# First four k-rows of x joined with three tiles' weights, and the last product summed onto a residual held in its banks

## The chip, the core and the metric

One core of one Trainium2 chip runs the kernel. The metric is the device time of one execution in microseconds (us). The kernel before takes 1969.95 us, the median of 3 runs (1969.86 to 1970.58). The profile is of one execution of its own, which took 1970.17 us; the span that the profile shows of it is 1968.4 us. Engines are named as in the profile: PE is TensorE's matmul, PEld its weight load, DVE VectorE, ACT ScalarE, POOL GpSimd, SP SyncE, which here only issues DMAs.

## What is computed

A hybrid encoder layer on 512 positions of 2048 channels: a norm, one input projection that feeds a convolution group and a 2-D neighbourhood attention, an output projection, and a gated MLP with a width-3 convolution, each with its residual; then a final norm.

```python
xn = rms_norm(x, attn_norm_g[l])
proj = jnp.einsum("bsd,dc->bsc", xn, w_in[l])
u_val, u_gate, q, k, v = jnp.split(proj, split_pts, axis=-1)
y_conv = conformer_conv(u_val, u_gate, conv_dw_w[l], conv_dw_b[l], conv_ln_g[l], conv_ln_b[l])
y_na = neighborhood_attention(heads(q), heads(k), heads(v), rpb[l])
...
x = x + jnp.einsum("bsc,cd->bsd", mixed, w_out[l])
xn = rms_norm(x, ffn_norm_g[l])
up = depthwise_conv(jnp.einsum("bsd,df->bsf", xn, w_up[l]), ffn_dw_w[l], ffn_dw_b[l])
gate, val = jnp.split(up, 2, axis=-1)
x = x + jnp.einsum("bsf,fd->bsd", jax.nn.silu(gate) * val, w_down[l])
...
return rms_norm(x, final_norm_g)
```

## The kernel before

Everything is float32. Each product is made of float32r matmuls of 128 x 128 weights against 512 moving columns. An operand is split into a high part (a copy cast to float32r, ACT) and a low part (the difference, DVE), and three matmuls, high by high, high by low and low by high, make one block's product. Weights come as units of 128 x 1024 (8 blocks, 512 KB): `raw_unit` loads one by a DMA from SP into one of 9 `raw` buffers, and `parts` splits it into `whi` (L136, ACT) and `wlo` (L137, DVE), 4 buffers each. `weights()` hands the units out in the order of the list `plan`, and makes them 3 ahead of their use.

The stages follow one another on PE: the 16 gate and value tiles and the attention's q, k and v tiles (`project`, L153 to L156, 48 matmuls a tile), the output projection (`out_half`), the up-projection (`up`, L745) and the down-projection (`product2`, L884). The last two are 2 x 2 block products in seven multiplications each.

**The start.** The input is scaled by `attn_norm_g` alone; the norm's factor `rstd` comes later and is multiplied onto the projected tiles. `first_glu` makes the first gate tile and the first value tile at once, in two PSUM banks, while x and the weights still arrive. x comes in 16 k-rows of 128 channels, the weights of the two tiles (`w_0`) in six pieces of 1, 1, 2, 4, 4 and 4 k-rows. SP issues x; ACT's own DMA queue brings the scale `g1` and the first three weight pieces (`we`), ahead of ACT's first instruction. Per k-row, `split_x` makes `xh` (L273, ACT) and `xl` (L274, DVE), and per piece `piece` makes the weights' two parts (L284, or L136 and L137). `pin` keeps these in the order of the code, so the order of the DMAs and splits at the start is written by hand. Ahead of it 11 matmuls of ones by ones (`WARM`, L124) run on PE. Then come the next gate tile's two units (`early`), and x once more with positions on partitions (`xn`, 8 loads of 512 KB), which ACT squares (L315) for the norm; `prm`, all other parameters, is loaded last. The norm's factor is a chain on DVE and ACT (`root_steps`) with two matmuls on PE at its end (`st`, L255).

**The end.** The last product (`product2(5, ...)`) makes the first half of the positions of half the columns, in four banks, i = 0 to 3: bank i holds rows i // 2 (128 positions each) and columns i % 2 (512 each). 18 of its 22 units run bank by bank within a unit; the last 4 units (`TAIL`) run bank after bank, 12 matmuls for each. Behind each bank `ready` adds it to `e3`, which holds the residual and the other products' shares (L935, DVE), squares the sum (L937, ACT) and multiplies by the final gain (L939, DVE; for i = 1 and 3, `fused`, the gain is left to `write`). Behind banks 1 and 3 `write` makes the norm's factor of 128 positions (L953 to L957), multiplies the four tiles with it (L963 on ACT, L965 and L967 on DVE) and issues their DMAs (L969). A scheduler orders instructions by priority within what the code's dependences allow; `shifted(-100)` moves this part ahead.

## Time and profile before

| | |
|---|---|
| time, median of 3 runs | 1969.95 us (1969.86 to 1970.58) |
| the profiled execution | 1970.17 us, span 1968.4 us |
| PE busy | 1956.4 us, 99% |
| PEld, DVE, ACT, POOL busy | 1665.2, 1608.1, 1100.9, 225.3 us |
| chain that ended last | PE 98% of the span |
| HBM read, written | 427.12 MB, 111.15 MB |

A row of the timeline gives the start (us from the span's start), the time from the first instruction's start to the last one's end, the engine, the line, the operation, the tile written and the tile read, and how many instructions were merged; in brackets how long the engine had been idle, and who ended that. A matmul's shown end lies behind the point at which the next one starts, so a run of n matmuls is as long as n - 1 starts and one duration. A row of the waits gives the total, the number and the longest of the waits. A row of a table of windows gives each engine's busy time and number of instructions in the stretch, then the granted clock, the DMA engines' busy share and the rate of their transfers. In answers on one tile or line, "DMA to landing" is the time from a transfer's issue until its semaphore says that all has arrived.

### The profile page before, as it was taken

To read this page: it belongs to the slowest core of one execution; us is meant where nothing else is said; L and a number is where in the kernel's file an instruction comes from. 1 tells how busy PE (TensorE), PEld (TensorE's weight loads), DVE (VectorE), ACT (ScalarE), POOL (GpSimd) and SP (SyncE) were. 2 spreads that over 40 slices of the span, in tenths; PEclk is the share of its full clock that TensorE was granted. 3 is DMA by queue.
4 is the path that set the end of the run, shared out by engine and by line. 5 is a ranking of instruction groups with operands and counts; after the bars stand their busy time and mean duration, and the time that the engine had idled before them with its cause. 6 is when DMAs were issued, how large, how long until landed. Compare 5 with 4: busy or idle time off the path is not lost.

```text
span 1968.4 us, 27634 instructions
## 1 busy us (share of the span) xinstructions
PE 1956.4 (99%) x10125; PEld 1665.2 (85%) x10125; DVE 1608.1 (82%) x2339; ACT 1100.9 (56%) x1766; POOL 225.3 (11%) x310
## 2 busy tenths in 40 slices
PE   9999999999999999999999999999999999999998
PEld 7888888888888888888888888888888888888886
DVE  5987687798557889898989898888888898885765
ACT  6244424448526666666666666666666644554654
POOL 0111111111001111111111111111110400000000
PEclk9999999999999999999999999999999999999999
DMA  9776766676858899999999999999986977666563
GB/s 363 182 196 173 187 178 185 179 190 203 258 147 213 206 251 244 271 246 272 236 274 245 268 242 269 242 270 246 265 229 168 387 242 233 217 214 193 192 201 120
DMA packets 141817, 447.83 MB, mean 228 GB/s; under 512 B 15088, under 2 KB 27632, under 8 KB 140272
## 3 DMA queue, kind: packets, MB, share of 16 engines
q1 hardware_dynamic: 88880, 290.31, 43.4%
q0 software_dynamic: 42624, 148.92, 35.3%
q10 hardware_dynamic: 10176, 6.83, 1.1%
q8 instruction: 80, 1.31, 0.3%
q14 instruction: 57, 0.47, 0.1%
HBM read 427.12 MB, written 111.15 MB: 273 GB/s over the span
## 4 chain that ended last, share of the span: by engine, by line
PE 98%; DVE 1%; DMA 0%; issue 0%; ACT 0%; ACTq 0%; DVEq 0%
PE pu L745 44%; PE pd L884 21%; PE pj L153 7%; PE pj L154 7%; PE pj L156 7%; PE po L153 3%; PE po L154 3%; PE po L156 3%; PE po L538 1%; PE sc L495 1%; PE pj L369 1%; PE trp L521 1%; DMA we<-in_w 0%; PE trx L640 0%; PE pj L373 0%
## 5 line engine op out<-in xcount | busy, mean ns | idle before, releaser
L136 ACT ACTIVATE whi<-raw 128x1024 fp32r<-128x1024 f32 x573 | 605.0, 1057 | 543.3 <-PE pj L154 154.7
L137 DVE TENSOR_TENSOR wlo<-raw,whi 128x1024 fp32r<-128x1024 f32 x573 | 699.3, 1221 | 235.4 <-ACT whi L136 196.3
L745 PE MATMUL pu<-xc,whi 128*128 128x512 f32 x2464 | 593.6, 391 | 0.0
L745 PEld LDWEIGHTS pu<-xc,whi 128*128 128x128 f32 x2464 | 451.3, 188 | 86.7 <-DVE xc L633 0.4
L745 PEld LDWEIGHTS pu<-xc,wlo 128*128 128x128 f32 x2464 | 319.2, 191 | 13.7
L745 PE MATMUL pu<-xc,wlo 128*128 128x256 f32 x2464 | 324.2, 283 | 0.0
L884 PE MATMUL pd<-whi,ho 128*128 128x512 f32 x1232 | 305.1, 389 | 0.1
L884 PEld LDWEIGHTS pd<-whi,ho 128*128 128x128 f32 x1232 | 231.1, 188 | 48.7 <-DVE vl L758 0.5
L153 PE MATMUL pj<-xh,whi 128*128 128x512 f32 x608 | 238.9, 393 | 0.0
L154 PE MATMUL pj<-xl,whi 128*128 128x512 f32 x608 | 236.8, 389 | 0.0
L395 DVE SCALAR_TENSOR_TENSOR y<-ch,prm,y 128x500 f32<-128x500 f32 (+14 forms) x240 | 177.2, 742 | 5.3
L884 PE MATMUL pd<-wlo,ho 128*128 128x512 f32 x616 | 165.1, 389 | 0.0
L156 PE MATMUL pj<-xh,wlo 128*128 128x512 f32 x608 | 150.3, 389 | 0.0
L153 PEld LDWEIGHTS pj<-xh,whi 128*128 128x128 f32 x608 | 114.1, 188 | 26.7 <-issue 2.8
L884 PEld LDWEIGHTS pd<-wlo,ho 128*128 128x128 f32 x616 | 115.6, 188 | 24.0
L156 PEld LDWEIGHTS pj<-xh,wlo 128*128 128x128 f32 x608 | 114.1, 188 | 23.7
L154 PEld LDWEIGHTS pj<-xl,whi 128*128 128x128 f32 x608 | 114.2, 188 | 23.5 <-issue 0.2
L754 ACT ACTIVATE pu<-pu 128x512 f32<-128x512 f32 x132 | 76.5, 580 | 92.9 <-PE pu L745 92.8
L694 POOL DMA_DIRECT2D raw<-in_w_up x88 | 78.0, 887 | 366.1 <-DVE wlo L137 143.9
L208 POOL DMA_DIRECT2D ws<-in_w_down x88 | 79.5, 903 | 301.5 <-DMA ws<-in_w_down 126.6
L205 POOL DMA_DIRECT2D ws<-ws x44 | 23.0, 524 | 317.9 <-PE pj L156 105.1
L205 POOL DMA_DIRECT2D ws<-in_w_down x44 | 23.2, 528 | 306.9 <-PE pj L156 174.5
(193 smaller groups left out, 1967.8 us busy)
## 6 DMA issues: line engine op xcount, KB each, us to landing
raw<-in_w_up SPq DMA_DIRECT2D x220, 512.0 KB, 5.9
ws<-in_w_down POOLq DMA_DIRECT2D x132, 512.0 KB, 6.3
raw<-in_w_up POOLq DMA_DIRECT2D x88, 512.0 KB, 7.3
raw<-ws SPq DMA_DIRECT2D x88, 512.0 KB, 3.6
raw<-in_w_in SPq DMA_DIRECT2D x76, 512.0 KB, 5.2
raw<-in_w_down SPq DMA_DIRECT2D x66, 512.0 KB, 4.1
ws<-ws POOLq DMA_DIRECT2D x44, 512.0 KB, 5.8
raw<-in_w_out SPq DMA_DIRECT2D x32, 512.0 KB, 4.7
```

Source lines behind the costliest of these rows:

```text
L136: i = nc.scalar.activation(hi[:, :n], raw[:, :n], AF.Copy)
L137: j = nc.vector.tensor_sub(lo[:, :n], raw[:, :n], hi[:, :n].bitcast(F32))
L153: nc.tensor.matmul(ps, hi, mh, start=first and k == 0, stop=False)
L154: nc.tensor.matmul(ps, hi, ml, start=False, stop=False)
L156: i = nc.tensor.matmul(ps, lo[:, wk * P:(wk + 1) * P], mh, start=False, stop=last and k == len(ws) - 1)
L205: behind(nc.gpsimd.dma_start(wsum[c][k], a), ins)
L208: nc.gpsimd.dma_start(wsum[c][k], w_down[k, {1: A21, 2: A11, 4: A11, 6: A12}[c]], accum_op=ALU.add, max_dma_last_dim=ROW)
L395: nc.vector.scalar_tensor_tensor(y[:, a:b], h[:, a + j - PAD:b + j - PAD], prm[:, o:o + 1], y[:, a:b], op0=ALU.mult, op1=ALU.add)
L694: nc.gpsimd.dma_start(a[c], w_up[f, q2], accum_op=ALU.add)
L745: i = nc.tensor.matmul(ps[:, :n], part[:, k * P:(k + 1) * P], comb[c][k][:, :n], start=j == 0 and not more, stop=j == 2 * U - 1, skip_grou ...
L754: nc.scalar.activation(to, ps, AF.Copy)
L884: m = nc.tensor.matmul(ps[i], h[:, o + t * P:o + (t + 1) * P], w[:, d], start=start and not more and kind == 0 and j == 0, stop=stop and k ...
```

## The change

The name of the change speaks first of narrow edge blocks in the attention. They stand in both kernels (`EDGE`, `KEYS`, `ATEDGE`), and the difference between the two holds nothing of the attention. It holds two things.

**The start.** `first_glu` makes three tiles at once, gate 0, value 0 and gate 1, the third in a bank of the pool that `project` uses; `glu(1)` then only projects its value tile. For the first four k-rows (`ROWS`) one array `xw` joins x's row, the three tiles' weights of that row and, in the first, the scale: one DMA each from SP (467 KB, then 459 KB three times). ACT issues no DMA at the start. The first row's splits are shared out: ACT makes half of `xh` and two tiles of `weh`, DVE the other half and one tile, and DVE copies the scale out. The other twelve k-rows come in pieces of two. Five of the eight `xn` loads and their squares stand among these pieces instead of behind them. Only the third tile's separate units (1 MB) fall away as such; value 1's two units are the `early` ones now. `WARM` is 8 instead of 11. `gated(0, ...)` is called at the end of `first_glu`, not behind the next unit.

**The end.** `prime` copies the four tiles of `e3` into four PSUM banks (ACT) during the product before, and the last product adds to what is there (`more` is True). `ready` then squares the bank itself (ACT) and multiplies the bank by the gain (DVE); the addition (L935) is gone for these four. `write` takes the primed bank for the fused tiles, and goes through the columns upwards.

```diff
-WARM = 11
+WARM = 8
+ROWS = 4
...
-    nc.scalar.dma_start(g1, par[:, :KD])
-    cuts = (0, 1, 2, 4, 8, 12, 16)
-    first = []
-    for k0, k1 in zip(cuts[:3], cuts[1:4]):
-        first.append(t2("we")[:, :2 * (k1 - k0) * P])
-        nc.scalar.dma_start(first[-1], w_0[:, 2 * k0 * P:2 * k1 * P])
...
+    for k in range(ROWS):
+        n = 3 * P
+        both = t4([P, S + n + KD], "xw")
+        m = S + n + (0 if k else KD)
+        pin(nc.sync.dma_start(both[:, :m], xw[k][:, :m]))
+        x, raw, lo = both[:, :S], both[:, S:S + n], t2("wel", F32R)[:, :n]
+        if k:
+            split_x(k, x)
+            his = [t2("weh", F32R)[:, :n]]
+            pin(nc.scalar.activation(his[0], raw, AF.Copy))
         else:
...
+            g = both[:, S + n:S + n + 1]
+            pin(nc.scalar.activation(h[:, :H], x[:, :H], AF.Copy, scale=g))
+            pin(nc.vector.tensor_copy(his[0], raw[:, :P]))
+            pin(nc.vector.tensor_scalar(h[:, H:], x[:, H:], g, None, op0=ALU.mult))
+            pin(nc.scalar.activation(his[1], raw[:, P:], AF.Copy))
+            pin(nc.vector.tensor_copy(g1, both[:, S + n:]))
+            pin(nc.vector.scalar_tensor_tensor(l, x, g, h.bitcast(F32), op0=ALU.mult, op1=ALU.subtract))
...
+    for p in range(ROWS // 2, KD // 2):
         x = t4([P, 2 * S], "x")
         pin(nc.sync.dma_start(x, xT[p]))
         for k in range(2):
             split_x(2 * p + k, x[:, k * S:(k + 1) * S])
...
+        piece(2 * p, 2 * p + 2)
+        if p > 2:
+            square(*todo.pop(0))
...
-        two = [psa.tile([P, S], F32, tag="tr", name="pj", bufs=2) for _ in range(2)]
+        three = [psa.tile([P, S], F32, tag="tr", name="pj", bufs=2) for _ in range(2)]
+        three.append(psm.tile([P, S], F32, tag="mm", name="pj"))
...
-        late.append(lambda: gated(0, *two))
+        gate.append(three[2])
+        gated(0, *three[:2])
...
-            add(x[i], x[i], ps[i])
+            if not whole:
+                add(x[i], x[i], ps[i])
+            src = ps[i] if whole else x[i]
             q = t2("sq")
-            nc.scalar.activation(q, x[i], AF.Square, accum_out=sq[th][:, t, o:o + 1])
+            nc.scalar.activation(q, src, AF.Square, accum_out=sq[th][:, t, o:o + 1])
             if i not in fused:
-                nc.vector.tensor_mul(x[i], x[i], gs[d])
+                nc.vector.tensor_mul(x[i], src, gs[d])
...
+    def prime(x):
+        primed.extend(four(True))
+        for a, b in zip(x, primed):
+            nc.scalar.activation(b, a, AF.Copy)
             yield
...
-                    nc.vector.scalar_tensor_tensor(x, x, y, gs[d], op0=ALU.mult, op1=ALU.mult)
+                    nc.vector.scalar_tensor_tensor(x, primed[i], y, gs[d], op0=ALU.mult, op1=ALU.mult)
...
-    steps += [ready(e0, a, 0, 1), ready(e1, a, 1, 1)]
+    steps += [ready(e0, a, 0, 1), ready(e1, a, 1, 1), prime(e3)]
...
-    a = four(True)
-    for i in product2(5, a, False):
+    for i in product2(5, primed, True):
```

How the order of instructions changes is shown at two places. The first is the start. SP's DMAs of before, from the first on (`raw<-in_w` are the two tiles' weights, `xn` the input once more):

```order
L292 DMA x<-in_xT 128x512 x2
L297 DMA x<-in_xT 128x1024 x2
L130 DMA raw<-in_w 128x1024
L297 DMA x<-in_xT 128x1024 x2
L130 DMA raw<-in_w 128x1024
L297 DMA x<-in_xT 128x1024 x2
L130 DMA raw<-in_w 128x1024
L297 DMA x<-in_xT 128x1024
L130 DMA raw<-in_w_in 128x1024
L309 DMA xn<-in_xn 128x1024 x4
```

SP's DMAs of the change, from the first on:

```order
L295 DMA xw<-in_xw 128x912
L295 DMA xw<-in_xw 128x896 x3
L320 DMA x<-in_xT 128x1024
L125 DMA raw<-in_w 128x768
L320 DMA x<-in_xT 128x1024
L125 DMA raw<-in_w 128x768
L286 DMA xn<-in_xn 128x1024
L320 DMA x<-in_xT 128x1024
L125 DMA raw<-in_w 128x768
L286 DMA xn<-in_xn 128x1024
```

The weights of the first rows, which came on ACT's queue, stand in SP's now, in one transfer with x, and the first `xn` stands ninth where it stood fourteenth. On PE, before, the first rows (`pj` are the projected tiles' banks, `weh` and `wel` the first weights' parts):

```order
L124 MATMUL warm<-ones 128x128 x11
L369 MATMUL pj<-xh,weh 128x512 x2
L369 MATMUL pj<-xl,weh 128x512 x2
L373 MATMUL pj<-xh,wel 128x512 x2
L369 MATMUL pj<-xh,weh 128x512 x2
L369 MATMUL pj<-xl,weh 128x512 x2
L373 MATMUL pj<-xh,wel 128x512 x2
```

PE's first rows of the change:

```order
L119 MATMUL warm<-ones 128x128 x8
L387 MATMUL pj<-xh,weh 128x512 x3
L387 MATMUL pj<-xl,weh 128x512 x3
L391 MATMUL pj<-xh,wel 128x512 x3
L387 MATMUL pj<-xh,weh 128x512 x3
L387 MATMUL pj<-xl,weh 128x512 x3
L391 MATMUL pj<-xh,wel 128x512 x3
```

Each k-row gives PE nine matmuls where it gave six, and three matmuls of ones are gone ahead of them. The second place is the end. DVE's last rows of before, from the last unit's split on (`xr` are the output's tiles, `pd` the banks):

```order
L935 TENSOR_TENSOR xr<-xr,pd 128x512
L954 TENSOR_SCALAR rsv<-sq,rsm 128x1
L955 SCALAR_TENSOR_TENSOR rsv<-rsr,rsv 128x1
L956 RECIPROCAL rsv<-rsv 128x1
L957 TENSOR_SCALAR rsy<-rsv,rsr 128x1
L965 SCALAR_TENSOR_TENSOR xr<-xr,rsy,g_15496 128x512
L967 TENSOR_SCALAR xr<-xr,rsy 128x512
```

DVE's last rows of the change:

```order
L975 TENSOR_SCALAR rsm<-rsm 128x1
L983 TENSOR_SCALAR rsv<-sq,rsm 128x1
L984 SCALAR_TENSOR_TENSOR rsv<-rsr,rsv 128x1
L985 RECIPROCAL rsv<-rsv 128x1
L986 TENSOR_SCALAR rsy<-rsv,rsr 128x1
L996 TENSOR_SCALAR xr<-xr,rsy 128x512
L994 SCALAR_TENSOR_TENSOR xr<-pd,rsy,g_15503 128x512
```

The addition of the last bank is gone ahead of the chain, and the two multiplications behind it have changed places. PE's last rows of before (banks 0 and 1 are the two halves of `pd_17413`, banks 2 and 3 are the other `pd`):

```order
L884 MATMUL pd_17413<-whi,ho 128x512 x8
L884 MATMUL pd_17413<-wlo,ho 128x512 x4
L884 MATMUL pd<-whi,ho 128x512 x4
L884 MATMUL pd_17413<-whi,ho 128x512 x8
L884 MATMUL pd_17413<-wlo,ho 128x512 x4
L884 MATMUL pd<-whi,ho 128x512 x4
L884 MATMUL pd<-wlo,ho 128x512 x4
L884 MATMUL pd<-whi,ho 128x512 x8
L884 MATMUL pd<-wlo,ho 128x512 x4
```

PE's last rows of the change:

```order
L903 MATMUL pd_17147<-whi,ho 128x512 x8
L903 MATMUL pd_17147<-wlo,ho 128x512 x4
L903 MATMUL pd<-whi,ho 128x512 x7
L903 MATMUL pd_17147<-whi,ho 128x512 x8
L903 MATMUL pd_17147<-wlo,ho 128x512 x4
L903 MATMUL pd<-whi,ho 128x512
L903 MATMUL pd<-wlo,ho 128x512 x4
L903 MATMUL pd<-whi,ho 128x512 x8
L903 MATMUL pd<-wlo,ho 128x512 x4
```

Seven matmuls of bank 2 stand between bank 0 and bank 1, where four did.

More of the change, by code (lines that the diff above doesn't have):

```diff
@@ L78, in layer @@
 @with_exitstack
-def layer(ctx: ExitStack, tc: tile.TileContext, xT, xn, w_0, w_in, w_out, w_up, w_down, par, tab, g3, out):
+def layer(ctx: ExitStack, tc: tile.TileContext, xT, xn, xw, w_0, w_in, w_out, w_up, w_down, par, tab, g3, out):
     nc = tc.nc
@@ L289, in layer, with piece @@
-    pieces, early = [], []
-    for k in range(2):
-        x = t2("x")
-        pin(nc.sync.dma_start(x, xT[0][:, k * S:(k + 1) * S]))
-        split_x(k, x)
-        pieces.append(piece(first[k], k, k + 1))
-    for p, at in ((1, 2), (2, 3), (3, 0), (4, 4), (5, 0), (6, 5), (7, 0)):
+    def piece(k0, k1):
+        n = 3 * (k1 - k0) * P
+        raw, i = raw_unit(w_0[:, 3 * k0 * P:3 * k1 * P], n)
+        pin(i)
+        w = parts(raw, n)
+        for i in w[2:]:
+            pin(i)
+        pieces.append((k0, k1, [w[0]], w[1]))
@@ L331, in stats1 @@
     def stats1():
-        for _ in range(3):
+        for _ in range(2):
             yield
@@ L927, in taken, with ready @@
             yield
-    def ready(x, ps, th, dh, only=range(2 * Q), fused=()):
+    def ready(x, ps, th, dh, only=range(2 * Q), whole=False, fused=()):
         for i in only:
@@ L957, in write @@
         nc.vector.tensor_scalar(y, v, r, 2.0, op0=ALU.mult, op1=ALU.mult)
-        for d in reversed(range(Q)):
+        for d in range(Q):
             for dh in range(2):
```

85 lines of the change are left out of this document (44 added, 41 removed).

## The prediction

> **What bounds the kernel now.** I read the page's busy times and chain first, then PE's waits, then the timeline of the two ends of the span, since the chain leaves nothing else to ask for.
>
> ```profile
> PE 1956.4 (99%) x10125; PEld 1665.2 (85%) x10125; DVE 1608.1 (82%) x2339; ACT 1100.9 (56%) x1766; POOL 225.3 (11%) x310
> PE 98%; DVE 1%; DMA 0%; issue 0%; ACT 0%; ACTq 0%; DVEq 0%
> ```
>
> PE is busy 1956.4 of 1968.4 us, and the chain is PE's. So 12.0 us are all that can be gained without taking work from PE, and the change takes only three matmuls of ones from it. The profiled execution's own time, 1970.17, is 1.8 above its span; I leave that as it is. PE's waits, all of them:
>
> ```profile
> PE pj L369 <- ACT weh L284: 1.8, 2, 1.3
> PE warm L124 <- DVE ones L119: 1.1, 1, 1.1
> PE st L264 <- DVE acc L226: 0.2, 1, 0.2
> ```
>
> That is 3.1 us. The rest of the 12.0 lies behind PE's last matmul, whose row is below: 1958.56 + 1.07 = 1959.63, so 8.8 us. The change works on both places. The start, row by row:
>
> ```profile
> 0.75 0.86 SPq L292 DMA_DIRECT2D x<-in_xT  x2
> 1.06 5.06 PE L124 MATMUL warm<-ones 128*128 128x128 f32 x22 [1.06 <-DVE ones L119]
> 5.02 0.75 DVE L274 SCALAR_TENSOR_TENSOR xl<-x,g,xh 128x512 fp32r<-128x512 f32 x1 [4.01 <-ACT xh L273]
> 5.14 0.42 ACT L284 ACTIVATE weh<-we 128x256 fp32r<-128x256 f32 x1 [0.15 <-DMA we<-in_w]
> 5.46 0.71 ACT L273 ACTIVATE xh<-x,g 128x512 fp32r<-128x512 f32 x1
> 5.69 0.42 DVE L284 TENSOR_TENSOR wel<-we,weh 128x256 fp32r<-128x256 f32 x1
> 5.78 0.82 PE L369 MATMUL pj<-xh,weh 128*128 128x512 f32 x2
> 6.44 0.63 PE L369 MATMUL pj<-xl,weh 128*128 128x512 f32 x2
> 39.27 1.98 PE L156 MATMUL pj<-xh,wlo 128*128 128x512 f32 x8
> 41.09 0.39 PE L255 MATMUL st<-dg,ones 128*128 128x512 f32 x1
> ```
>
> A matmul takes a slot of (1.98 - 0.39) / 7 = 0.227 us. Ahead of the first `st` at 41.09 stand 96 matmuls of the first two tiles and 48 of the third, 144 x 0.227 = 32.7 us. Had they run unbroken they would have begun at 8.4. That is the start's price before, late first matmul and waits in one number.
>
> **The start after the change.** The same 144 matmuls come first, now nine per k-row. What decides is when the first can start, at what pace, and whether the data keep up.
>
> *Landing.* `xw`'s first transfer (467 KB) is SP's first, at 0.75. The first table is of x's own loads at the start, 256 KB the smallest; the second of 512 KB weight loads in a quiet stretch (1870 to 1912); then the rates of two stretches.
>
> ```profile
> DMA to landing us min/median/max: 3.3/6.4/8.0
> DMA to landing us min/median/max: 3.4/3.6/4.0
> 0.00:10.00 10.00, 7.60 (x33) 6.82 (x34) 2.96 (x6) 4.84 (x8) 0.70 (x6) 1.00 0.78 281
> 20.00:30.00 10.00, 10.00 (x46) 8.28 (x45) 4.88 (x7) 8.20 (x13) 0.00 (x0) 1.00 1.02 400
> ```
>
> At best it takes the 3.3 us of half its size, at worst that and 211 KB more at 281 GB/s, 4.05 us. I take 3.6, the median of the nearest size: landed at 4.35 (4.05 to 4.8).
>
> *Splits.* The first matmul needs one weight tile and both halves of `xh`. DVE makes the tile (128 columns) and a half (256) one after the other, at most twice the 0.42 of the 256-column row and nearer 0.6; ACT its half and then two weight tiles, 0.42 each. With a semaphore's delay the first matmul starts at 5.0, the second may at 5.25. `xl` is ready 0.9 later, at 5.9, the low weights by 6.5. At 0.227 a slot that costs 0.2 us of waiting; at half the pace none.
>
> *Pace.* The 22 records of ones take 5.06 us, (5.06 - 0.42) / 21 = 0.22 each for 128 columns, whereas 512 columns take 0.227 later. The first real pair takes 0.82, its second starting 0.43 behind its first (0.82 - 0.39); the next pair takes 0.63. So the array ran at half pace until about 6.0, although the clock column says 1.00. Before, this cost nothing: the second row's weights were awaited anyway. Now the matmuls from 5.0 to 6.0 go at half pace and lose 0.5. The start's price is then 5.0 + 0.5 = **5.5 instead of 8.4, a gain of 2.9**. Eight matmuls of ones end at 1.06 + 16 x 0.22 = 4.6, so PE also pauses 0.4 us.
>
> The Trainium skill, page "TensorE: Matmul & The Clock Gate", section "Part 1: The HAM clock gate (the "warmup" mystery)", says that the array gets its full clock after one sustained busy window of about 3.4 us, and that the windows run freely. The trace agrees, with full pace 4.9 us behind the first matmul. By the page it could come between 4.5 and 7.9, and a pause inside a window speaks against the shorter warm-up; the price would be 5.2 to 6.5 and the time 1965.6 to 1966.8.
>
> *Keeping up.* A k-row holds PE for 9 x 0.227 = 2.04 us. It needs 459 KB, 1.15 us at 400 GB/s and 1.6 at 281; on ACT at most 2 x 0.71, on DVE at most 2 x 0.75 (what 512 columns take). The second row lands by 6.0 and is split on ACT by 7.4; the first ends at 7.5. From the fifth row on a pair of rows holds PE for 4.09 us against 917 KB and one 512 KB `xn`, 3.6 us. No wait.
>
> *The norm's factor.* The list of transfers up to `prm` grows from 11.89 to 12.94 MB.
>
> ```profile
> 35.16 0.23 DVE L680 TENSOR_SCALAR fwn<-prm 128x132 f32<-128x132 f32 x1 [3.56 <-DMA prm<-in_par]
> 39.61 0.48 DVE L251 TENSOR_SCALAR dg<-ident,rsv 128x128 fp32r<-128x128 f32 x2
> ```
>
> `prm` landed at 35.1 and the chain behind it ended at 40.1, 5.0 us. Now it lands 1.05 / 0.4 = 2.6 later, at 37.7, and the chain ends by 42.7. The first `st` stands behind 176 matmuls, at 5.5 + 40.0 = 45.5, so it is covered by 2.8 us. SP's queue alone carries all of it now; ACT's is empty at the start, so nothing of `xw` shares the engines with a later transfer.
>
> **The end after the change.** The end of bank 0, the wait between banks 0 and 1, and the rows around the last bank:
>
> ```profile
> 1950.23 1.07 PE L884 MATMUL pd<-wlo,ho 128*128 128x512 f32 x4
> ...
> 1952.08 1.69 PEld L884 LDWEIGHTS pd<-whi,ho 128*128 128x128 f32 x8 [0.29 <-DVE xr L935]
> 1958.42 1.32 ACT L963 ACTIVATE xr<-xr,rsy 128x512 f32<-128x512 f32 x2
> 1958.56 1.07 PE L884 MATMUL pd<-wlo,ho 128*128 128x512 f32 x4
> 1959.16 0.95 ACTq L969 DMA_DIRECT2D out_T<-xr  x2
> 1959.91 0.68 DVE L935 TENSOR_TENSOR xr<-xr,pd 128x512 f32<-128x512 f32 x1
> 1960.62 0.63 ACT L937 ACTIVATE sq<-xr 128x512 f32<-128x512 f32 x1 [0.88 <-DVE xr L935]
> 1961.37 0.29 ACT L953 ACTIVATE rsr<-sq,rsm 128x1 f32<-128x1 f32 x1
> 1962.40 0.75 DVE L965 SCALAR_TENSOR_TENSOR xr<-xr,rsy,g 128x512 f32<-128x512 f32 x1
> 1963.07 0.48 DVE L967 TENSOR_SCALAR xr<-xr,rsy 128x512 f32<-128x512 f32 x1
> 1963.18 0.81 SPq L969 DMA_DIRECT2D out_T<-xr  x2
> ```
>
> Bank 1's matmuls waited 0.29 us for the addition that reads bank 0, in the same tile. Its readers are now the square (0.63 on ACT) and the product with the gain (0.68 on DVE), side by side, and seven matmuls (1.59 us) stand in between instead of four (0.91): no wait. Bank 0 ended at 1950.23 + 1.07 = 1951.30; 36 slots behind it make 8.17 us, so the last bank ends at 1959.47 instead of 1959.63. The square starts there instead of 1960.62: the addition is gone, and so is DVE's delay ahead of it. ACT must by then be through bank 1's two scalings and two DMA issues, which ended at 1960.1 (1959.16 + 0.95); DVE's chain for them had the additions of banks 1 and 2 (0.68 each) in its way, and without them, but with the seven matmuls ahead of bank 1 instead of four (0.5 later), they come some 0.85 earlier, at 1959.25. So the chain's next step moves from 1961.37 to 1960.25, **1.1 earlier**, and all behind it, since its instructions are the same. The two multiplications swap: SP's first write goes out after 0.48, not 0.75, at 1961.8 instead of 1963.18, the second 1.05 earlier, ACT's two 1.1 earlier. The last 1 MB of writes then ends 1.05 to 1.4 earlier; I take 1.2.
>
> **Between.** PE's order there is the same, so each wait that it could get is a new one. `prime` adds four ACT copies, 0.6 each, where `ready` works:
>
> ```profile
> 1850.00:1860.00 10.00, 10.00 (x45) 8.27 (x45) 10.00 (x16) 8.01 (x16) 0.00 (x0) 1.00 0.60 189
> 1871.55 1.06 ACT L136 ACTIVATE whi<-raw 128x1024 fp32r<-128x1024 f32 x1 [1.66 <-PE pd L884]
> ```
>
> DVE is full and ACT at 80% there, but by 1871 ACT waits for PE again to free a buffer, so the splits had not fallen behind; they are made 3 units (8.2 us) ahead. Queued behind a copy on ACT are those splits alone. Cost nothing, 2.4 us at most without that cover.
>
> **The sum.** 2.9 + 1.2 = 4.1 us off the profiled execution's 1970.17: 1966.1. That execution was 0.2 above the median of 1969.95, so **1965.9**. A change within 0.2% (3.9 us) is about what a measurement of this kernel can't tell from none, so the forecast lies on that edge. Ends: start 0.9 to 3.5 (rivals 1 and 2), end 1.05 to 1.4.
>
> **Rivals.**
> 1. *The pause restarts the wait for full pace.* Then it would come 4.9 us behind 5.0, and half pace loses 2.5, not 0.5: 1967.9. For it: the pause is new; against it: it is a tenth of the time. Chance 0.15.
> 2. *Earlier data, full pace at the first matmul.* Landing at 4.05, price 4.9, end 1.4: 1965.0. Chance 0.13.
> 3. *Part of it does nothing.* The attention isn't touched, so nothing comes from there; and if the copies of `prime` do stall PE by 2.4 us, 1968.3. Against it: the 1.66 us above. Chance 0.08.
> 4. *Slower: the norm's factor becomes the wait.* PE stands at `st` if `prm` lands behind 40.5, that is if the start's 12.94 MB take a mean rate under 325 GB/s from 0.75 on, and the gain is gone at 44.6. At 260 GB/s: landing 50.5, chain to 55.5, a wait of 10: 1975.9. For it: the first 10 us ran at 281 GB/s, against it: before, the 11.89 MB came at 346 GB/s (to 35.1), and the stretch from 20 to 30 at 400. Chance 0.04.
>
> The forecast itself has 0.60, its own spread 1965.2 to 1966.7; 0.42 of it lies beyond 0.2%. Faster by over 0.2%: 0.42 + 0.13 = 0.55. Within: 0.18 + 0.15 + 0.08 = 0.41. Slower: 0.04. The range 1964.8 to 1967.9 takes in rivals 1 and 2.
>
> **What would show it.** First `pj` at 4.8 to 5.3, no wait of PE on `weh` or `whi` behind it, the first `st` at 45 to 46 without a wait, no wait on DVE between the last banks, the last square straight behind the last matmul, PE idle some 9.4 us in all (the first 1.1, a pause of 0.4, the 0.2 at L264, 7.7 at the end). A first matmul behind 5.5, pairs at 0.82 beyond 8 us, or a wait at `st` would make it wrong.

## The result, and the profile after

The changed kernel takes **1966.61 us**, the median of 20 runs (1966.27 to 1967.52), beside 1969.95 us of the kernel before in 20 runs on the same chip (1969.46 to 1970.58). The ratio is 0.9984, 95% interval 0.9978 to 0.999: 3.3 us or 0.17% faster, on the inner side of the 0.2% on whose edge the forecast lay. The prediction was 1965.9, in a range from 1964.8 to 1967.9. The profiled execution took 1966.36 us, with a span of 1964.6.

The page after: the engines' busy times, and the chain that ended last.

```profile
PE 1954.8 (100%) x10119; PEld 1664.3 (85%) x10119; DVE 1606.0 (82%) x2341; ACT 1102.5 (56%) x1772; POOL 225.7 (11%) x310
PE 99%; DVE 1%; issue 0%; ACT 0%; DVEq 0%
```

PE is idle for 1964.6 - 1954.8 = 9.8 us instead of 12.0. Its waits after (total, number, longest) have lost the row on the first rows' weights, 1.8 us:

```profile
PE warm L119 <- DVE ones L114: 1.1, 1, 1.1
PE st L259 <- DVE acc L221: 0.2, 1, 0.2
```

The start after, from the timeline: SP's four issues, the ones, the first row's splits, the first nine matmuls, and then the first matmul of the next tile and the first `st`.

```profile
0.75 1.81 SPq L295 DMA_DIRECT2D xw<-in_xw  x4
1.06 3.71 PE L119 MATMUL warm<-ones 128*128 128x128 f32 x16 [1.06 <-DVE ones L114]
4.15 0.23 DVE L306 CAST weh<-xw 128x128 fp32r<-128x128 f32 x1 [3.14 <-DMA xw<-in_xw]
4.15 0.51 ACT L305 ACTIVATE xh<-xw 128x256 fp32r<-128x256 f32 x1 [1.91 <-DMA xw<-in_xw]
4.79 0.97 PE L387 MATMUL pj<-xh,weh 128*128 128x512 f32 x3
5.59 0.94 PE L387 MATMUL pj<-xl,weh 128*128 128x512 f32 x3
6.37 0.85 PE L391 MATMUL pj<-xh,wel 128*128 128x512 f32 x3
...
37.65 0.39 PE L148 MATMUL pj<-xh,whi 128*128 128x512 f32 x1
...
44.91 0.39 PE L250 MATMUL st<-dg,ones 128*128 128x512 f32 x1
```

The joined row is there at 4.15 and the first real matmul (the first on `pj`) runs at 4.79 instead of 5.78. The matmul at 37.65 is the first behind the 144, so the start's price in this execution is 37.65 - 144 x 0.227 = 5.0 instead of 8.4. Three matmuls of 0.227 a slot take 0.39 + 2 x 0.227 = 0.84 us at full pace; the first three take 0.97, the third group 0.85. Full pace was there almost at once.

The end after: the end of bank 0 and its readers, the wait in front of bank 1, and the rows around the last bank.

```profile
1946.78 1.07 PE L903 MATMUL pd<-wlo,ho 128*128 128x512 f32 x4
...
1947.89 0.60 ACT L958 ACTIVATE sq<-pd 128x512 f32<-128x512 f32 x1 [2.57 <-PE pd L903]
1948.61 0.69 DVE L960 TENSOR_TENSOR xr<-pd,g 128x512 f32<-128x512 f32 x1 [2.03 <-ACT sq L958]
...
1955.15 1.07 PE L903 MATMUL pd<-wlo,ho 128*128 128x512 f32 x4
...
1956.26 0.60 ACT L958 ACTIVATE sq<-pd 128x512 f32<-128x512 f32 x1 [0.76 <-PE pd L903]
...
1958.01 1.34 ACT L992 ACTIVATE xr<-xr,rsy 128x512 f32<-128x512 f32 x2 [0.73 <-DVE rsy L986]
...
1958.76 0.95 ACTq L998 DMA_DIRECT2D out_T<-xr  x2
```

PE's weight load has one wait in the last 17 us:

```profile
PEld pd L903 <- DVE xr L960: 0.3, 1, 0.3
```

The last matmul ends at 1955.15 + 1.07 = 1956.22, where it was 1959.63: 3.4 earlier, all of it from the start. The square follows at once (1956.26), and the chain behind it is shorter: ACT's two last writes are issued from 1958.76, 2.54 behind the last matmul, where before it was 3.52 (1963.15). And yet the span ends 1964.6 - 1956.2 = 8.4 us behind the last matmul, where before it was 8.8: 0.4 less, not 1.2. What became longer is the writes themselves. From issue to landing, the eight last writes of `xr` took, least, median and most, in the kernel before:

```profile
DMA to landing us min/median/max: 2.2/2.8/3.5
```

and in the change:

```profile
DMA to landing us min/median/max: 2.5/3.2/4.1
```

So two questions were open: why the last writes are slower after a change at the other end of the program, and how much of the start's 3.4 us is there in every execution.

### The profile page after: what moved, and what is told of

It is laid out like the page before. It is cut to its first block, busy times and chain, and to the rows that moved or that the text cites. A ratio compares the mean times of both kernels' runs of the same rounds, so it can differ in the third digit from the quotient of the medians.

```text
span 1964.6 us, 27635 instructions
## 1 busy us (share of the span) xinstructions
PE 1954.8 (100%) x10119; PEld 1664.3 (85%) x10119; DVE 1606.0 (82%) x2341; ACT 1102.5 (56%) x1772; POOL 225.7 (11%) x310
## 4 chain that ended last, share of the span: by engine, by line
PE 99%; DVE 1%; issue 0%; ACT 0%; DVEq 0%
PE pu L764 44%; PE pd L903 21%; PE pj L148 7%; PE pj L149 7%; PE pj L151 7%; PE po L148 3%; PE po L149 3%; PE po L151 3%; PE pj L387 1%; PE po L557 1%; PE sc L514 1%; PE pj L391 1%; PE trp L540 1%; PE trx L659 0%; DVE acc L221 0%
## 5 line engine op out<-in xcount | busy, mean ns | idle before, releaser
L131 ACT ACTIVATE whi<-raw 128x1024 fp32r<-128x1024 f32 (+1 forms) x574 | 604.4, 1055 | 539.0 <-PE pj L149 147.2
L132 DVE TENSOR_TENSOR wlo<-raw,whi 128x1024 fp32r<-128x1024 f32 (+1 forms) x574 | 698.8, 1218 | 231.9 <-ACT whi L131 196.1
L148 PE MATMUL pj<-xh,whi 128*128 128x512 f32 x592 | 232.7, 393 | 0.0
L149 PE MATMUL pj<-xl,whi 128*128 128x512 f32 x592 | 230.6, 390 | 0.0
L151 PE MATMUL pj<-xh,wlo 128*128 128x512 f32 x592 | 146.3, 389 | 0.0
```

The lines of the kernel that those rows point to most:

```text
L131: i = nc.scalar.activation(hi[:, :n], raw[:, :n], AF.Copy)
L132: j = nc.vector.tensor_sub(lo[:, :n], raw[:, :n], hi[:, :n].bitcast(F32))
L148: nc.tensor.matmul(ps, hi, mh, start=first and k == 0, stop=False)
L149: nc.tensor.matmul(ps, hi, ml, start=False, stop=False)
L151: i = nc.tensor.matmul(ps, lo[:, wk * P:(wk + 1) * P], mh, start=False, stop=last and k == len(ws) - 1)
```

## The experiments

Twelve kernels ran in four groups, each beside the kernel before, whose median was 1969.72 to 1969.99. The table gives what the sections below use. The interval of a ratio is about 0.0009 to either side, 1.8 us, so the medians alone don't settle differences of a few tenths between two variants; these are read from the profiles, and one profile is one execution. The fifth column is the stretch from PE's last matmul to the end of the span. "Full pace" is the time at which the trace's record of PE's clock goes from half to full. The last column is the slowest of the eight last writes.

| kernel | median us | first real matmul | full pace | stretch | slowest write |
|---|---|---|---|---|---|
| before | 1969.95 | 5.78 | 6.03 | 8.77 | 3.5 |
| the change | 1966.61 | 4.79 | 4.59 | 8.36 | 4.1 |
| start alone | 1967.86 | 4.64 | 5.61 | 9.45 | 4.2 |
| end alone | 1968.59 | 5.78 | 6.02 | 7.56 | 3.2 |
| columns downwards | 1966.81 | 4.78 | 6.74 | 8.45 | 4.2 |
| banks apart | 1966.25 | 4.82 | 5.89 | 8.38 | 4.1 |
| before, spare input | 1970.21 | 6.14 | 4.81 | 8.91 | 3.8 |
| scale by ACT's queue | 1966.78 | 5.04 | 6.12 | 8.31 | 4.1 |
| 11 ones | 1967.03 | 4.90 | 3.91 | 8.39 | 4.1 |
| 4 ones | 1968.60 | 4.89 | 8.91 | 8.35 | 4.1 |
| before, sizes of after | 1969.66 | 6.08 | 6.26 | 8.87 | 3.7 |
| sizes of before | 1967.06 | 5.07 | 6.08 | 8.29 | 4.0 |
| rows not joined | 1967.02 | 4.79 | 6.66 | 8.15 | 4.1 |
| fetch moved | 1966.25 | 5.07 | 6.32 | 7.75 | 3.4 |

### The two halves apart

One kernel has the change's start with the end of before, one the start of before with the change's end. The edit of the first, against the change, without the lines of `write`, which goes through the columns downwards again and takes no bank (the second is the same lines the other way round, in the kernel before):

```diff
-            if not whole:
-                add(x[i], x[i], ps[i])
-            src = ps[i] if whole else x[i]
+            add(x[i], x[i], ps[i])
...
-                nc.vector.tensor_mul(x[i], src, gs[d])
+                nc.vector.tensor_mul(x[i], x[i], gs[d])
...
-    steps += [ready(e0, a, 0, 1), ready(e1, a, 1, 1), prime(e3)]
+    steps += [ready(e0, a, 0, 1), ready(e1, a, 1, 1)]
...
-    for i in product2(5, primed, True):
+    a = four(True)
+    for i in product2(5, a, False):
```

The theory from the two profiles alone was that the start carries nearly all of the gain and the end only 0.4. The rival was that each is worth what the prediction gave it.

> The change's start with the end of before. Theory (start carries nearly all): the profile after shows the start 3.4 us cheaper and the end only 0.4, so this run is 3.0 to 3.4 below before, within 0.5 of the change. Rival (the prediction's split, 2.9 and 1.2): it is 2.1 below before, 1.2 above the change.

> The start of before with the change's end. Theory: 0.2 to 0.6 below before; from PE's last matmul to the end of the span some 8.4 us, not 8.8. Rival (the prediction's split): 1.2 below before, 7.7 us behind the last matmul.

The start alone takes 1967.86 us (1967.3 to 1968.46), ratio 0.999 (0.9982 to 0.9999); the end alone 1968.59 (1968.38 to 1968.94), ratio 0.9994 (0.9985 to 1.0003). Beside 1969.72 of the kernel before these are 1.9 and 1.1 us, together 3.0: the theory fell, and the rival, 2.1 and 1.2, was near. (The executions agree: the kernel before took 1969.41 or more in all 33, the end alone 1968.94 or less in all 11.) The end alone is worth what was predicted, the start less than PE shows: PE's last matmul comes 3.25 earlier with the new start (1956.38 against 1959.63), but the stretch behind it grows from 8.77 to 9.45. That leaves 2.6 between the two profiles, where the medians have 1.9. Part of the rest is that before's profile had drawn a dear start: by its first `st`, which stands behind the 144 matmuls, its price was 8.4; in the three other profiles with the start of before the first `st` stands at 40.62, 41.00 and 40.33, a price of 7.9, 8.3 and 7.6, so 8.1 is the mean of the four. The writes tell of the longer stretch. The end alone:

```profile
DMA to landing us min/median/max: 2.2/2.7/3.2
```

The start alone:

```profile
DMA to landing us min/median/max: 2.5/3.2/4.2
```

The old end with the new start has slow last writes, the new end with the old start has quick ones. So the writes' length hangs on what came with the start, not on the end.

### Two details of the end

Both against the change: `write` goes through the columns downwards as before, and banks 1 and 2 of `primed` are exchanged.

```diff
-        for d in range(Q):
+        for d in reversed(range(Q)):
```

```diff
-        primed.extend(four(True))
+        b = four(True)
+        primed.extend((b[0], b[2], b[1], b[3]))
```

> The change, but the last tiles are scaled and written from the last column down, as before. Theory (the new order of the writes makes them land later, which cost 0.6 of the end's gain): 0.3 to 0.6 below the change, the last writes landing in 2.8 us again. Rival (the later landing is chance of one profiled execution): within 0.2 of the change.

> The change, with the last product's second and third bank exchanged, so that bank 1 doesn't lie in one tile with bank 0 and has nothing to wait for. Theory: PE's wait on DVE ahead of bank 1 (0.34 on the weight load) is gone, the last matmul ends 0.2 earlier, and the time falls by 0.2. Rival (the wait is hidden by another): no change of the last matmul's end against its first.

The columns downwards take 1966.81 us (1966.32 to 1967.55), ratio 0.9985 (0.9976 to 0.9994), the banks apart 1966.25 (1966.03 to 1967.15), ratio 0.9983 (0.9974 to 0.9992). The columns' order is worth 0.1 us of the stretch (8.45 against 8.36), and the slowest write stays at 4.2, so it isn't the order that makes the writes slow: the rival held. With the banks apart PE's weight load has no wait between the last banks, and bank 1's matmuls follow bank 0's at 1948.06, 0.9 us ahead of the start of the product with the gain:

```profile
1947.15 1.07 PE L903 MATMUL pd<-wlo,ho 128*128 128x512 f32 x4
1947.84 1.77 PEld L903 LDWEIGHTS pd<-whi,ho 128*128 128x128 f32 x8
1948.06 1.98 PE L903 MATMUL pd<-whi,ho 128*128 128x512 f32 x8
...
1948.98 0.69 DVE L960 TENSOR_TENSOR xr<-pd,g 128x512 f32<-128x512 f32 x1 [2.03 <-ACT sq L958]
```

So the change's 0.3 us wait is a matter of which tile the next bank lies in, and the last bank ends 1956.38 - 1948.22 = 8.16 us behind bank 0, as the prediction had it. The two medians differ by 0.6 us, but these two profiles also got full pace at 6.74 and 5.89, and PE's last matmul ends at 1957.03 and 1956.38.

### Pace

Two kernels change the number of ones, `WARM`, to 11 and to 4.

> The change with 11 matmuls of ones instead of 8. If the pause ahead of the first real matmul is harmless and full pace comes at a time of its own (4.6 to 6.7 us in the profiles so far), the three only stand in the way: at half pace they end at 5.9, at full pace from 4.6 on at 5.3; first pj at 5.3 to 5.9 instead of 4.8, price of the start up by 0.4 to 0.6 us, time 1966.8 to 1967.4. If the pause delays full pace, 11 without a pause bring it earlier, below 5 us, and the time stays within 0.2 us of the change's or falls below it.

> The change with 4 matmuls of ones instead of 8: they end at 2.9, so PE pauses 1.9 us ahead of the first real matmul instead of 0.2. If the pause restarts the wait for full pace (rival 1 of the prediction), pairs of matmuls stay at half pace until 8.2 or later, and the time rises by 1 to 2 us over the change's, to 1967.6 to 1968.6. If full pace only hangs on a time since PE began, it comes at 4.6 to 6.7 as before, and the time is within 0.3 us of the change's.

With 11 it takes 1967.03 us (1966.47 to 1967.96), ratio 0.9986 (0.9977 to 0.9994), with 4 1968.60 (1968.2 to 1970.14), ratio 0.9994 (0.9985 to 1.0003). PE's rows with 11 ones:

```profile
1.06 4.06 PE L119 MATMUL warm<-ones 128*128 128x128 f32 x22 [1.06 <-DVE ones L114]
4.90 0.96 PE L387 MATMUL pj<-xh,weh 128*128 128x512 f32 x3
```

and with 4:

```profile
1.06 2.08 PE L119 MATMUL warm<-ones 128*128 128x128 f32 x8 [1.06 <-DVE ones L114]
4.89 1.62 PE L387 MATMUL pj<-xh,weh 128*128 128x512 f32 x3 [1.75 <-DVE g L309]
6.31 1.48 PE L387 MATMUL pj<-xl,weh 128*128 128x512 f32 x3
7.59 1.47 PE L391 MATMUL pj<-xh,wel 128*128 128x512 f32 x3
```

With 11 the median is what the first theory gave: a harmless pause and three matmuls that only stand in the way; the profile is what the second gave, full pace below 5 us, at 3.91. The eleven executions fall into two groups, six at 1966.5 to 1967.0, to which the profiled one belongs, and five at 1967.7 to 1968.0, so this run doesn't settle between the two. With 4, behind a pause of 1.9 us, the whole first row goes at half pace, and full pace comes at 8.91, 4.0 us behind the first real matmul. That is rival 1 of the prediction, with a longer pause, and it costs 2.0 us. With 8 ones, where PE pauses for 0.4 us at most, no profile has full pace behind 6.74. The eight profiles with the new start and 8 ones have full pace at 4.59 to 6.74, 6.0 on the mean, 3.5 to 5.7 us behind the first matmul. Where it falls differs from execution to execution: the kernel with the columns downwards does the same at the start as the change, and its first rows read

```profile
4.78 1.62 PE L387 MATMUL pj<-xh,weh 128*128 128x512 f32 x3
6.20 1.12 PE L387 MATMUL pj<-xl,weh 128*128 128x512 f32 x3
7.15 0.86 PE L391 MATMUL pj<-xh,wel 128*128 128x512 f32 x3
```

It is 0.8 us behind the change's profile from the third group on (7.15 against 6.37), and PE's last matmul ends 0.8 later too. The change's profiled execution had an early one. On the mean of the eight the first real matmul is at 4.88 and half of the 1.12 us from there to 6.0 is lost, which makes 5.4; read at the first matmul behind the 144, the price in the eight is 4.96 to 6.04, 5.5 on the mean, and 5.3 in the four that load the first rows as the change does.

The record of PE's clock shows where the spread comes from. Full pace lasts 1952.42, 1955.84 or 1959.25 us in the fourteen profiles, which is 572, 573 or 574 times 3.413, so it begins and ends on a grid of 3.41 us, and each execution meets that grid at another point. The 3.41 us ahead of full pace held 0.56 us without work for PE with 11 ones (from 0.50 to 3.91; PE begins at 1.06) and 0.44 with the fetch moved (from 2.90 to 6.32, with the pause behind the ones), and this was no obstacle. The step ahead of that held 1.1 us without work with the columns downwards (from -0.08 to 3.33), and with 4 ones the step from 2.09 to 5.50 held 2.0, and full pace did not come. So a short pause is harmless and one of 1.9 us costs a whole step. This is a reading of the records; no run tested it apart.

### The rows not joined

The change with x's row, the scale and the weights of the first four rows loaded by a DMA each, 9 issues instead of 4.

```diff
-        pin(nc.sync.dma_start(both[:, :m], xw[k][:, :m]))
+        pin(nc.sync.dma_start(both[:, :S], xT[k // 2][:, k % 2 * S:(k % 2 + 1) * S]))
+        if not k:
+            pin(nc.sync.dma_start(both[:, S + n:], par[:, :KD]))
+        pin(nc.sync.dma_start(both[:, S:S + n], w_0[:, 3 * k * P:3 * (k + 1) * P]))
```

> The change with the joined rows taken apart: SP loads x's row, the scale and the three tiles' weights by a DMA each, 9 issues instead of 4 for the first four rows, everything else alike. An issue takes SP 0.45 us (4 in 1.81), so the first row's weights are issued 0.9 later. If joining is what the early start hangs on, first pj comes at 5.4 to 5.8 instead of 4.8, PE waits again on a second row, and the time rises by 0.5 to 0.9 us over the change's, to 1967.1 to 1967.5. If the transfers' own time decides (smaller ones land sooner), first pj stays at 4.6 to 5.1 and the time within 0.2 us of the change's.

It takes 1967.02 us (1966.52 to 1968.89), ratio 0.9987 (0.9978 to 0.9995), 0.4 above the change, between the two expectations. The profile's start fits the second of them:

```profile
1.65 0.42 SPq L297 DMA_DIRECT2D xw<-in_w  x1
...
4.15 0.23 DVE L308 CAST weh<-xw 128x128 fp32r<-128x128 f32 x1 [3.14 <-DMA xw<-in_w]
...
4.79 1.62 PE L389 MATMUL pj<-xh,weh 128*128 128x512 f32 x3
```

The weights, issued 0.9 later and smaller, are there at the same 4.15, and the first matmul comes at the same 4.79. PE doesn't wait. Joining brings nothing here that the profile shows; what is left for the start's gain is the order of the rows and the third tile, which no run took apart. Full pace came at 6.66 in this profile, 0.66 behind the mean of 6.0, and at half pace that is 0.3; whether the 0.4 between the medians is more than such draws isn't shown.

### Why the last writes are slower: the theories

A: the sizes of the inputs (`xw` is new, `w_0` half as large again) decide. B: chance. C: what the start does on the queues. D, formed later: which SBUF buffers the last tiles get. The last one, F, follows below; none is called E. First, an unread array of `xw`'s size in the kernel before, and, in the change, the scale on ACT's queue:

```diff
-    arrays = {"xT": xT, "xn": np.ascontiguousarray(a["x"][0]), "w_0": w_0, "w_in": w_in,
+    xw = np.zeros((4, P, S + 3 * P + KD), np.float32)
+    arrays = {"xT": xT, "xn": np.ascontiguousarray(a["x"][0]), "xw": xw, "w_0": w_0, "w_in": w_in,
```

```diff
+    nc.scalar.dma_start(g1, par[:, :KD])
...
-            pin(nc.vector.tensor_copy(g1, both[:, S + n:]))
```

> The kernel before, with one more input array in DRAM of xw's size that nothing reads. The four kernels with the change's start end their profile 8.4 to 9.5 us behind PE's last matmul, the two with the start of before 8.8 (old end) and 7.6 (new end), so with equal ends the new start has cost 0.7 to 0.85 us at the other end of the program. Theory A, the extra array shifts where the output lies in HBM: the stretch from PE's last matmul to the end of the span grows from 8.77 to about 9.5, the time by some 0.7 us (1970.4 to 1970.6 where before is 1969.8). Theory B, the length of the last writes varies from execution to execution: any stretch from 8.0 to 9.5, the time within 0.3 us of before. Theory C, it hangs on what the new start does on the queues: stretch 8.8, time as before.

> The change, but the scale g1 is loaded by a DMA of 8 KB on ACT's queue at the start, as before, instead of being copied out of the first joined row. Theory C, the queue of ACT that is first used at the end of the program pays for it there: the stretch behind PE's last matmul falls from 8.4 to 7.6, the time by 0.7 us, to 1965.6 to 1966.0. Theory B (variation) and theory A (place in HBM): time as the change's, 1966.3 to 1966.9, the stretch anywhere from 7.5 to 8.5. The start loses nothing by it: first pj at 4.6 to 5.0.

They take 1970.21 us (1969.66 to 1970.68), ratio 1.0001 (0.9993 to 1.001), and 1966.78 (1966.57 to 1967.5), ratio 0.9984 (0.9975 to 0.9993), the latter with its first matmul at 5.04, just behind the 4.6 to 5.0 expected. The stretch with the scale on ACT's queue stays at 8.31, so it isn't that this queue is first used at the end; chance is out as well, since the change, the scale by ACT, 11 ones and 4 ones all show 4.1 us for the slowest write and 8.31 to 8.39 for the stretch. The spare array did a little: the median of the last writes is 3.1 instead of 2.8, the slowest 3.8 instead of 3.5.

Then the sizes both ways. The kernel before got `xw`'s size and 1 MB of unread rows behind `w_0`; the change got inputs of before's number and sizes, its joined rows standing in tiles of `w_in` that it no longer reads.

```diff
+    w_0 = np.concatenate([w_0, w_0[:P // 2]])
```

```diff
-        pin(nc.sync.dma_start(both[:, :m], xw[k][:, :m]))
+        pin(nc.sync.dma_start(both[:, :m], w_in[k // 2 * NC_, :, k % 2 * 1024:k % 2 * 1024 + m]))
```

> The kernel before, on inputs of the change's sizes in DRAM: an unread array of xw's size and 1 MB of unread rows behind w_0's. Nothing that runs is changed. The nine profiles so far show what follows PE's last matmul always alike for one start: with the change's start one or two of the last writes land 0.6 to 0.9 us behind the rest. Theory A, the sizes of the inputs decide by where the output lies in HBM: this kernel ends as the one with the change's start and the old end did, 9.3 to 9.5 us behind PE's last matmul instead of 8.8, the last writes 4.1 to 4.2 us at most from issue to landing instead of 3.5; time 1970.4 to 1970.8 where before is 1969.9. Theory D, the buffers in SBUF that the new start's rotation gives to the last tiles decide, or the queue's state: 8.8 us, 3.5 us, time as before.

> The change on inputs of before's number and sizes: the joined rows stand in two tiles of w_in that the change doesn't read any more, the end of w_0's rows in a third. The same instructions and buffers as the change. Theory A: the stretch behind PE's last matmul falls from 8.4 to 7.5 us, the slowest of the last writes from 4.1 to 3.2 us, and the time by 0.7 us, to 1965.6 to 1966.1. Theory D: 8.4 us, 4.1 us and 1966.3 to 1966.9, as the change.

They take 1969.66 us (1969.46 to 1970.03), ratio 0.9999 (0.999 to 1.0008), and 1967.06 (1966.6 to 1969.31), ratio 0.9987 (0.9979 to 0.9996). Neither theory was right. The sizes do something: on the sizes of before the median of the change's last writes falls from 3.2 to 2.7, as in the end alone, and on the sizes of the change that of the kernel before rises from 2.8 to 3.1. But there the last completion comes only 0.2 later (7.84 us behind PE's last matmul, not 7.66), and in the change the slowest stays:

```profile
DMA to landing us min/median/max: 2.2/2.7/4.0
```

The rate of the transfers from PE's last matmul to the end of the span, in 40 slices, shows what is left. The change:

```profile
GB/s 371 371 312 400 234 312 322 410 322 312 234 146 29 0 0 341 390 400 342 371 322 390 312 215 361 361 419 410 303 88 10 0 0 0 0 0 0 0 0 0
```

The change on the sizes of before:

```profile
GB/s 355 424 365 356 385 395 365 365 405 346 10 0 0 0 0 326 375 434 326 355 424 355 405 365 375 385 375 395 148 39 10 0 0 0 0 0 0 0 0 0
```

The dips (234, 215) are gone with the sizes, and a thin tail of 39 and 10 remains: nearly all has arrived, and the end waits for a little. Of the last 48 completions 47 come by 6.47 us behind PE's last matmul, and one at 7.19. In this stretch the table of DMA queues has one packet of another kind, a fetch of instructions of 8 KB:

```profile
q14 instruction: 1, 0.01, 0.2%
```

In a slice of 0.207 us its 8 KB are those 39 GB/s, and the 10 behind it are one packet of 2 KB. On the sizes of before the fetch runs from 6.03 to 6.33; that packet runs from 6.33 to 6.42, where all other data have arrived by 6.04. The fetch starts 5.75 to 6.75 us behind PE's last matmul, among the writes, in eight of the nine profiles with the new start above, and 7.2 to 8.6 us behind it, later than the writes, in the four with the start of before. The ninth is that of the rows not joined, with 2.6.

What goes with it is SP: the trace has 1238 SP instructions with the old start, 1244 with the new one, and 1249 with the rows not joined. **Theory F**: SP's stream reaches the point where the next block is fetched 6 instructions sooner, and the fetch falls among the last writes. The traces bear out that it is SP's: in every profile this last fetch starts when SP has started 1232 to 1237 of its instructions, and in the change fetches stand at SP's 593, 721, 851, 976 and 1105 instructions too, some 128 apart.

The last kernel has SP's loads of the final gain in quarters, 12 more instructions long before the end, on the sizes of before and with the banks apart.

```diff
-            nc.sync.dma_start(gs[d], g3[:, d * S:(d + 1) * S])
+            for p in range(4):
+                o = p * S // 4
+                nc.sync.dma_start(gs[d][:, o:o + S // 4], g3[:, d * S + o:d * S + o + S // 4])
```

> The change with three edits: banks 1 and 2 exchanged, so that neighbouring groups at the end lie in different double banks; inputs of before's number and sizes; and 12 more DMAs on SP's queue long before the end (each of the four loads of the final gain in quarters). What the packets of the runs so far show: with the sizes of before, all of the last writes but one land by 6.5 us behind PE's last matmul, against 7.0 with the change's; and one lands 0.7 us behind the rest wherever an instruction fetch of 8 KB starts 6.0 to 6.8 us behind PE's last matmul, among the writes (it starts at 7.2 to 8.6, behind them, in the kernels with the start of before, whose SP has 6 instructions less; at 2.6 in the one with 5 more). Theory F, the fetch is SP's and its transfer holds up one DMA engine: with 12 more instructions on SP it comes before the last writes, the straggler is gone, the slowest write takes 3.2 to 3.4 us instead of 4.0, the stretch behind PE's last matmul is 7.5 to 7.7 us instead of 8.3, and the time 1965.4 to 1966.2, depending on when full pace comes. If the straggler has another cause, it stays: 8.3 us, 4.0 us, and 1966.2 to 1967.0.

It takes 1966.25 us (1965.87 to 1966.68), ratio 0.9982 (0.9973 to 0.9991). No fetch is left behind PE's last matmul, the thin tail is gone, and so is the slow write:

```profile
GB/s 378 399 357 126 0 0 0 0 0 0 0 0 0 0 0 0 231 378 431 368 336 389 420 368 357 399 389 347 389 378 200 0 0 0 0 0 0 0 0 0
```

```profile
DMA to landing us min/median/max: 2.2/2.8/3.4
```

All completions are in at 6.41 us behind the last matmul, as in the end alone (6.39), and the stretch is 7.75. Theory F is borne out. The banks' exchange doesn't do it: alone (the banks apart) it leaves the last completion at 7.28, where the change has 7.27. With the rows not joined, where the sizes are the change's and the fetch is early, at 2.6, four profiles make a square, though they differ in other lines too (the last completion behind PE's last matmul, us):

| | sizes of before | sizes of the change |
|---|---|---|
| fetch elsewhere | 6.41 (fetch moved) | 6.88 (rows not joined) |
| fetch among the last writes | 7.19 (sizes of before) | 7.27 (the change) |

The sizes alone cost 0.5, the fetch alone 0.8, both together 0.9: what comes last counts. Of the stretch, which is what the time has, it is a little less: 7.75, 8.15, 8.29 and 8.36, so 0.4, 0.5 and 0.6. The time, 0.8 below the sizes of before, is just above what theory F expected, and the stretch of 7.75 too. The joined rows, read out of `w_in`, land at 4.43 and 4.44 instead of 4.15 in the two kernels on the sizes of before, and the first matmul comes 0.3 us later. No version tried lies measurably below the change; this one and the banks apart are lowest.

The Trainium skill, page "Runtime: NRT & Kernel Launch", section "Instruction fetch mechanics", says that each sequencer fetches its next block over a DMA queue of its own while it executes, and that the cost is mostly hidden. The profiles agree that the fetches have queues apart from the data's, and show blocks of 16 KB, the page's size, on q8 alone, and of 8 KB on q14; a cost of it shows here only at the end. The Trainium skill, page "DMA: Bandwidth & Descriptors", section "Why a DMA increments its semaphore by 16 and not by 1", has it that a transfer is done when the last of up to 16 engines has written; the one late completion of 48 is what that looks like.

## Why the prediction came out as it did

**The forecast time was 0.7 us too low, and the term that failed is the end's.** It said that the chain's next step moves 1.1 earlier "and all behind it, since its instructions are the same", and took 1.2 for the last writes. Alone the end brought that: 1.1 in time, 1.2 in the stretch, completions at 6.39 instead of 7.66 us behind the last matmul. In the change 0.4 was left of it, since the writes themselves became slower by 0.9 (7.27), by an instruction fetch and by the inputs' sizes, both brought by the start. The prediction looked at the writes' issues alone and took their length as given. With 2.9 for the start, 2.9 + 0.4 is the 3.3 measured, but that it fits so closely is partly luck: 2.9 counts from the 8.4 of one execution, the dearest of four. From the means of the profiles the start gave 8.1 - 5.5 = 2.5, or 2.8 with the four that load as the change does, and the sum is 2.9 to 3.2.

**Landing, splits, first matmul: right.** 4.15 for 4.35, 4.79 for 5.0.

**Pace: right on the mean.** Full pace at 6.0 was the forecast and is the mean of eight profiles; the price of the start was put at 5.5 and is 5.5 there, 5.0 in the change's own profile, which is rival 2's situation (price 4.9). That the forecast took 6.0 from the one profile of before and met the mean is luck in part, since single profiles have it at 4.59 to 6.74. Rival 1 (the pause) did not occur at 0.4 us and less, and does at 1.9.

The Trainium skill's free-running window, page "TensorE: Matmul & The Clock Gate", section "Part 1: The HAM clock gate (the "warmup" mystery)", fits the spread better than one fixed time does: by it 4.5 to 7.9 was to be expected, and 4.59 to 6.74 was seen. The trace agrees on the window's length, with the grid of 3.41 us. With 11 ones it came at 3.91, 2.85 us behind the first matmul, sooner than the page's 3.4 us; that the 0.56 us without work ahead of it counted as part of the window would explain it.

**Keeping up: right.** No wait of PE on x or weights.

**The norm's factor: right, with more cover than worked out.** `prm` landed at 37.1 instead of 37.7, and the chain behind it was through by 40.9, 4.0 us ahead of the first `st` at 44.91:

```profile
37.14 0.23 DVE L699 TENSOR_SCALAR fwn<-prm 128x132 f32<-128x132 f32 x1 [1.02 <-DMA prm<-in_par]
40.06 0.87 DVE L246 TENSOR_SCALAR dg<-ident,rsv 128x128 fp32r<-128x128 f32 x4
```

**No wait between bank 0 and bank 1: wrong.** The square and the product were to run side by side. The product waits for the square (2.03 us idle, released by ACT's square), ends at 1949.30, and PE's wait stays at 0.3. So the last bank ended 8.37 us behind bank 0, not 8.17. It cost 0.2 of the sum, and with the banks apart it is 8.16. The Trainium skill, page "PSUM — Partial Sum Buffer", section "PSUM bank collisions raise a hardware error", says that two engines must not touch the same bank at once, two reads included, and that the compiler's scheduler keeps them apart: the order seen here agrees with that, and the prediction had missed it.

**`prime` costs nothing: right.** PE's waits show no new row in the product where it runs, and from the start of the up-projection's first matmul to that of the last one of all it is 1280.13 us before (from 679.11) and after (from 675.70).

**What would show it**: the first `st` came at 44.91 instead of 45 to 46, for the early full pace of that execution; the wait between the last banks was there; the last square did follow straight; PE's idle time was 9.8 us instead of 9.4, 8.4 of it behind the last matmul instead of 7.7.

## What to carry over

A transfer at the very end of a program is as long as its slowest engine takes, so look at its landings, not only at its issues: here a few instructions more at the start put an instruction fetch among the last writes. Where a gain of a few us at a start is forecast, take the mean of full pace's arrival over executions, since one profile shows one draw of 4.6 to 6.7 us; the same goes for the start that it is compared with (7.6 to 8.4). Two engines that read the same PSUM bank are to be counted one behind the other (0.72 us here), and the next bank written should lie in another tile (0.3 us).

## What was not expected of the hardware

- An instruction fetch of 8 KB (0.31 us of one DMA engine) among the last 1 MB of writes held up the end; 12 more instructions on SP took that away (stretch 8.29 to 7.75, time 1967.06 to 1966.25, with the banks' exchange among the edits). The packets show 0.38 of that 0.8: the one packet behind the fetch ends at 6.42, the others by 6.04. Why its completion then follows 0.77 behind it, where without a fetch the last one follows 0.35 to 0.46 behind the last data, is open.
- The sizes of the inputs changed how long the last writes take (median 3.2 against 2.7 us, 3.1 against 2.8 in the kernel before), though nothing in the program writes differently there. That it is the output's place in HBM is only argued.
- The joined rows landed at 4.15 from an array of their own, and at 4.43 and 4.44 out of rows of 8 KB in `w_in`. The cause was not looked for.
- Full pace came 2.85 to 5.7 us behind the first matmul with a pause of at most 0.4 us, and 4.0 us behind the first matmul that followed a pause of 1.9.
